# Planner delays of weight sums, down operands and norm statistics in a two-layer trunk

## The chip, the cores and the metric

The kernel runs on one core of one Trainium2 chip. The metric is the device time of one launch in microseconds (us). The kernel before has a median of 2538.11 us over 3 runs (2534.14 to 2538.69). One further execution was recorded by the hardware profiler; it took 2531.58 us, and its trace is what the rows below are read from.

## The reference, cut to what matters

Two layers work on `x` of 1024 tokens by 1024 channels in float32. Each layer adds three terms in turn: a mixer, an attention to a memory of 256 tokens, and a gated feed-forward block; a last RMSNorm ends the trunk.

```python
# even layer: short gated convolution beside causal pooling;  odd layer: mLSTM beside latent attention
x = x + mixer(rmsnorm(x, norm_mix_g))
x = x + memory_cross_attention(rmsnorm(x, norm_xattn_g), mem_n, wq, wkv, wo)
g, u = split(rmsnorm(x, norm_ffn_g) @ w_gate_up)     # 1024 -> 2 * 2816
x = x + (silu(g) * u) @ w_down                       # 2816 -> 1024
```

## The kernel before, in words

`x` stays on chip, transposed: 8 blocks of 128 channels for each of two token halves of 512. Every product of matrices is made of matmuls of 128 by 128 by 512, and each stands three times: operands are split in a high part (`whi` of a weight, `xgh`, `xth`, `fh` of an activation) and a low remainder (`wlo`, `xgl`, ...), and `mm3` (its matmuls are recorded at L267) adds high by high, high by low and low by high.

A weight takes a fixed path. SP loads a raw tile of 256 KB (`fetch`, L331) into one of five buffers `wraw`; ScalarE (ACT) writes `whi` (L344); VectorE (DVE) writes `wlo` = `wraw` - `whi` (L345), which frees the raw buffer for the next load. Some weights are sums of two tiles. Such a sum is an accumulating DMA on the queue of GpSimd (POOL), L339, onto a raw tile that is already there, either out of HBM (`in_ffn_...`) or out of another raw tile (`wraw<-wraw`). It starts when both tiles are there, and only when it has landed can ACT and DVE split the tile.

The feed-forward block runs 22 column blocks j in pairs of products by a form with seven products in place of eight. One period of two j's has three stages on TensorE (PE): a gate and up stage of 84 matmuls, G1 (j odd), another, G2 (j even), and the down stage D of 84 matmuls (`Down.out`), which adds into `x` by 28 DVE additions (L204), four for each of the seven products. In each stage two weights are loaded sums out of HBM (s1 and s3) and two are sums of these with other tiles (s2 after s1, s4 after s2). DVE and ACT also make, in the same stretch, the gate (L2038 copies a psum, L2042 scales, L2044 is SiLU, L2046 scales, L2053 multiplies by up) and the operands of the next down stage: `Down.build` forms seven right-hand operands `11`, `t1`, `t2`, `21`, `t3`, `22`, `t4` of two finished j's, and `parts` splits each by an ACT copy (L138) and a DVE subtraction (`fh`, L139). The products in D come in the order 11, 12, s2, s1, s3, s4, 22.

The order of instructions on each engine is written by a planner in Python (`Threads`). Parts of the program are generators that `yield` either a delay in planned nanoseconds or an event; a matmul moves the planner's clock on, and of the generators that are due the one with the lowest rank writes its next instructions. The delays decide only where an instruction stands in its engine's queue; on the chip each engine takes its queue in order and waits by semaphores. Three rules matter here. `pair_blocks.landed` says when a sum may be split while splits are still ahead of need: 4500 planned ns after its DMA was written for s2 and s4, 5500 for s1 and s3; if a product needs the weight, `must` splits at once. `self.ahead` is how many split weights may stand ready (3 inside the feed-forward block, 2 elsewhere). And `D1`, `D2` delay the statistics of a norm: `norm_stats` sums squares on PE (`ssq`), makes the reciprocal root by small DVE operations (L473 to L478), copies it to `ncol` (L530), and D2 later broadcasts it to rows on PE (`rbp`, L271) and ACT (`rb`, L537). The event `col_ev`, also D2 later, lets the cross attention start (L1827).

Around the FFN these rules act in three other places. In the even layer's mixer the pooling waits for `rb` (L790 on DVE, then a chain of POOL additions L796, then `pd` L805 on DVE, then the matmul `pps`). In the odd layer's mixer `rb` scales `qk` (L1247). In the cross attention, the attention itself and the down stage share DVE.

Of the kernel before, what the change touches and what calls it, by code (L numbers as in the profile page):

```python
# [115 lines left out]
class Down:  # L116
# [36 lines left out]
    def build(self, c):  # L153

        t = self.t

        def tile(i, h):
            while (c, i, h) not in self.full:
                yield 500
            return self.full[c, i, h]  # L160

        def operand(nm, src, fresh=True):
            if self.pace and fresh:
                yield self.pace / 2
            yield (self, 2)
            self.right[c, nm] = self.parts(src, self.eng)
            t.th.set(self.ev[c][nm], 2500)
            if self.pace:
                yield self.pace / 2 if fresh else self.pace

        b11 = yield from tile(0, 0)
        if self.pace:
            yield self.over[c - 1]
        yield from operand("11", b11, False)
        b12 = yield from tile(0, 1)
        t.nc.vector.tensor_sub(b11, b11, b12)
        yield from operand("t1", b11)
        b22 = yield from tile(1, 1)
        t.nc.vector.scalar_tensor_tensor(b11, b11, -1.0, b22, op0=ALU.mult, op1=ALU.subtract)
        yield from operand("t2", b11)  # L180
        b21 = yield from tile(1, 0)
        yield from operand("21", b21, False)
        t.nc.vector.tensor_sub(b12, b22, b12)
        yield from operand("t3", b12)
        yield from operand("22", b22, False)
        t.nc.vector.scalar_tensor_tensor(b11, b11, -1.0, b21, op0=ALU.mult, op1=ALU.subtract)
        yield from operand("t4", b11)

# [33 lines left out]
class Trunk:  # L222
# [4 lines left out]

    D1, D2, D3 = 15000, 6000, 20000  # L230
    PARTS = ((0, slice(0, HT)), (1, slice(0, 256)), (1, slice(256, HT)))
    BUFS = {"xg": 32, "g": 20, "o": 8, "p": 7, "pt": 4, "r": 4, "rb": 2}
    RAWS = 5
# [136 lines left out]
    def pair_blocks(self, order, eng):  # L370


        names, raw, step, at = deque(("s1", "11", "12", "s3", "22")), {}, {}, {}
        th = self.th
        reads = {"s1": 2, "11": 3, "12": 2, "s3": 1, "22": 1}

        def get(nm):
            while nm not in raw:
                self.fetch()
                raw[names[0]], step[names[0]], at[names[0]] = self.raws.popleft()  # L380
                names.popleft()
                self.held += 1
            return raw[nm]

        def read(nm):
            reads[nm] -= 1
            if not reads[nm]:
                self.held -= 1

        def add(nm, place, other):  # L390
            src = get(other)
            before = [step[other]] if step.get(other) else []
            step[nm] = step[place] = self.add_to(raw[place], src, 3500 if before else 1000, before)
            raw[nm] = raw[place]
            emit = step[nm].emit
            step[nm].emit = lambda: (emit(), read({"s2": "11"}.get(other, other)))

        def landed(nm):
            s = step.get(nm)
            if s is None:  # L400
                return th.now >= at[nm] + 3500
            return s.out is not None and th.now >= s.out + (4500 if nm in ("s2", "s4") else 5500)

        for nm in order:
            tile = get(nm)
            while not self.must and not landed(nm):
                yield None
            if step.get(nm):
                step[nm].flush()
            self.split_w(tile, eng)  # L410
            read({"s2": "11", "s4": "12"}.get(nm, nm))
            if nm == "11":
                add("s2", "11", "s1")
            elif nm == "12":
                add("s4", "12", "s2")
            yield False
# [83 lines left out]
    def late_stats(self, N, h, rows):  # L500

        nc, acc = self.nc, None
        yield 3000
        for t in self.xT[h]:
            sq = self.g("p" if acc else "pt", name="sq")
            nc.scalar.activation(sq, t, AF.Square)
            if acc is None:
                acc = sq
            else:
                nc.vector.tensor_add(acc, acc, sq)  # L510
            yield 800
        yield from self.norm_stats(N, h, acc, rows, (self.D1 if rows else self.D3) - 9400)

    def norm_half(self, N, h, gname, off=0, rows=True):

# [1739 lines left out]
```

## Time and profile before

| What | Value |
|---|---|
| median of 3 runs | 2538.11 us |
| the profiled execution | 2531.58 us, its span 2529.9 us |
| PE, matmuls | 2473.7 us busy, 98% of the span, 12029 instructions |
| DVE | 1955.1 us, 77% |
| ACT | 1082.3 us, 43% |
| POOL | 450.9 us, 18% |
| DMA, HBM read | 176.84 MB |

Busy time of matmuls overlaps, since they are pipelined: a matmul of 512 columns lasts about 0.39 us in the trace, and the next one starts about 0.23 us after it. A short wait of PE can therefore hide inside the busy time, and waits are read from the distance between starts. The chain that ended last is PE for 75%, DVE for 13% and DMA for 4%.

### The profile page before, as it was taken

The page shows a single profiled execution, that of the slowest core. Times are in us where ns is not written, and L with a number is a line of the kernel's source. Part 1 is how long each engine was busy: PE and PEld are TensorE (multiplying, and loading weights), DVE is VectorE, ACT ScalarE, POOL GpSimd, SP SyncE. Part 2 cuts the span into 40 slices and gives each one's busy share as a digit, 9 for nine tenths or more (in the row PEclk, how much of TensorE's full clock was granted, in tenths as well). Part 3 has the DMA queues.
Part 4 walks back from the last instruction along what each step waited for, and adds up shares of the span by engine and source line. Part 5 has one row for each costly group of instructions (what it writes and reads, how often), then busy time and mean ns, then how long its engine had stood idle before and what let it go on. Part 6 is the DMA issues. An engine that isn't in the chain of part 4 may idle for free.

```text
span 2529.9 us, 34429 instructions
## 1 busy us (share of the span) xinstructions
PE 2473.7 (98%) x12029; PEld 2027.8 (80%) x12029; DVE 1955.1 (77%) x3789; ACT 1082.3 (43%) x2125; POOL 450.9 (18%) x487
## 2 busy tenths in 40 slices
PE   9999999999999999999999999999999999999998
PEld 7788888777777777779998788788777777777777
DVE  5777779988888887774638788787998777888887
ACT  5322555533333333343324367575554333333333
POOL 5411021121222122110000120001111212121222
PEclk9999999999999999999999999999999999999999
DMA  5232212455555555511122132122135555555552
GB/s 139 54 83 81 92 47 58 87 120 121 118 122 117 115 125 122 116 42 39 39 50 55 31 81 72 46 84 51 45 80 122 118 115 117 117 122 120 119 119 97
DMA packets 300093, 227.33 MB, mean 90 GB/s; under 512 B 28911, under 2 KB 250320, under 8 KB 299920
## 3 DMA queue, kind: packets, MB, share of 16 engines
q1 hardware_dynamic: 226688, 150.28, 20.5%
q0 software_dynamic: 72912, 74.32, 18.9%
q8 instruction: 95, 1.56, 0.3%
q14 instruction: 78, 0.64, 0.1%
q10 hardware_dynamic: 320, 0.53, 0.1%
HBM read 176.84 MB, written 4.19 MB: 72 GB/s over the span
## 4 chain that ended last, share of the span: by engine, by line
PE 75%; DVE 13%; DMA 4%; issue 4%; ACT 3%; POOL 1%; SPq 0%; DVEq 0%; ACTq 0%; POOLq 0%
PE gu L267 25%; PE pj L267 14%; PE dn L267 12%; PE op L267 6%; DVE x L204 4%; PE tp L267 4%; DMA wraw<-wraw 3%; DVE wlo L345 3%; PE as L267 2%; PE ao L267 1%; DMA wraw<-in_ffn_w_down_dram 1%; DVE fh L139 1%; PE apt L271 1%; PE o L267 1%; PE kps L267 1%
## 5 line engine op out<-in xcount | busy, mean ns | idle before, releaser
L344 ACT CAST whi<-wraw 128x512 fp32r<-128x512 f32 (+1 forms) x652 | 398.8, 617 | 929.4 <-DMA wraw<-wraw 207.7
L345 DVE TENSOR_TENSOR wlo<-wraw,whi 128x512 fp32r<-128x512 f32 (+1 forms) x652 | 442.2, 686 | 176.4 <-ACT whi L344 170.4
L267 PE MATMUL dn<-fh,whi 128*128 128x512 f32 x1456 | 459.9, 397 | 14.7 <-DVE x L204 11.0
L204 DVE TENSOR_TENSOR x<-x,dn 128x512 f32<-128x512 f32 x728 | 451.5, 677 | 0.3 <-PE dn L267 0.2
L267 PEld LDWEIGHTS dn<-fh,whi 128*128 128x128 f32 x1456 | 266.1, 188 | 100.8 <-issue 22.8
L267 PE MATMUL dn<-fh,wlo 128*128 128x512 f32 x728 | 286.0, 393 | 0.0
L267 PE MATMUL gu<-xth,whi 128*128 128x512 f32 x672 | 267.2, 398 | 8.9 <-DVE f L2063 3.1
L267 PE MATMUL gu<-xtl,whi 128*128 128x512 f32 x672 | 264.9, 394 | 0.7 <-DVE xtl L286 0.7
L267 PE MATMUL gu<-xth,wlo 128*128 128x512 f32 x672 | 265.0, 394 | 0.0
L267 PE MATMUL pj<-xgh,whi 128*128 128x512 f32 x592 | 238.7, 403 | 2.1 <-DVE x L204 2.1
L267 PE MATMUL pj<-xgl,whi 128*128 128x512 f32 x592 | 231.3, 391 | 0.0
L267 PE MATMUL pj<-xgh,wlo 128*128 128x512 f32 x592 | 231.3, 392 | 0.0
L267 PE MATMUL gu<-xgh,whi 128*128 128x512 f32 x568 | 224.1, 394 | 0.2
L267 PE MATMUL gu<-xgh,wlo 128*128 128x512 f32 x568 | 222.0, 391 | 0.0
L267 PE MATMUL gu<-xgl,whi 128*128 128x512 f32 x568 | 221.7, 390 | 0.0
L339 POOL DMA_DIRECT2D wraw<-in_ffn_w_gate_up_dram x84 | 116.1, 1382 | 509.1 <-DVE x L204 119.6
L339 POOL DMA_DIRECT2D wraw<-wraw x136 | 124.9, 918 | 390.0 <-DVE wlo L345 141.4
L267 PEld LDWEIGHTS dn<-fh,wlo 128*128 128x128 f32 x728 | 136.7, 188 | 31.2
L267 PEld LDWEIGHTS gu<-xth,whi 128*128 128x128 f32 x672 | 126.7, 189 | 42.8 <-ACT f L2038 8.3
L267 PEld LDWEIGHTS gu<-xtl,whi 128*128 128x128 f32 x672 | 126.9, 189 | 29.2 <-DVE xtl L286 1.6
L267 PEld LDWEIGHTS gu<-xth,wlo 128*128 128x128 f32 x672 | 126.9, 189 | 29.1
L267 PEld LDWEIGHTS pj<-xgh,whi 128*128 128x128 f32 x592 | 111.7, 189 | 25.8 <-issue 2.7
(494 smaller groups left out, 4736.5 us busy)
## 6 DMA issues: line engine op xcount, KB each, us to landing
wraw<-in_ffn_w_gate_up_dram SPq DMA_DIRECT2D x218, 256.0 KB, 3.0
wraw<-wraw POOLq DMA_DIRECT2D x136, 256.0 KB, 3.4
wraw<-in_ffn_w_down_dram SPq DMA_DIRECT2D x108, 256.0 KB, 2.8
wraw<-in_ffn_w_gate_up_dram POOLq DMA_DIRECT2D x84, 256.0 KB, 5.1
wraw<-in_od_w_in_dram SPq DMA_DIRECT2D x42, 256.0 KB, 2.8
wraw<-in_ffn_w_down_dram POOLq DMA_DIRECT2D x40, 256.0 KB, 4.5
wraw<-in_ev_w_in_dram SPq DMA_DIRECT2D x32, 256.0 KB, 2.6
wraw<-in_xattn_wkv_dram SPq DMA_DIRECT2D x32, 256.0 KB, 2.7
```

Source lines behind the costliest of these rows:

```text
L139: eng.tensor_sub(lo, src, hi.bitcast(F32))
L204: getattr(nc.vector, op)(x, x, ps)
L267: self.nc.tensor.matmul(out, lhsT, rhs, start=start, stop=stop, skip_group_check=onto)
L271: self.nc.tensor.transpose(out, src, self.ident[:k, :k])
L339: return Step(self.th, lambda: self.nc.gpsimd.dma_start(out=raw, in_=src, accum_op=ALU.add), delay, before)
L344: self.nc.scalar.copy(hi, raw)
L345: (eng or self.nc.vector).tensor_sub(lo, raw, hi.bitcast(F32))
```

## The change

Delays of the planner change. No operation is added or taken away.

```diff
-        def operand(nm, src, fresh=True):
-            if self.pace and fresh:
+        def operand(nm, src):
+            if self.pace:
                 yield self.pace / 2
             yield (self, 2)
             self.right[c, nm] = self.parts(src, self.eng)
             t.th.set(self.ev[c][nm], 2500)
             if self.pace:
-                yield self.pace / 2 if fresh else self.pace
+                yield self.pace / 2
...
-        yield from operand("11", b11, False)
+        yield from operand("11", b11)
...
-    D1, D2, D3 = 15000, 6000, 20000
+    D1, D2, D3 = 15000, 8500, 20000
...
-            return s.out is not None and th.now >= s.out + (4500 if nm in ("s2", "s4") else 5500)
+            return s.out is not None and th.now >= s.out + (4500 if len(self.ready) < 2 else 8000)
...
-        yield from self.norm_stats(N, h, acc, rows, (self.D1 if rows else self.D3) - 9400)
+        yield from self.norm_stats(N, h, acc, rows, (self.D1 + 2500 if rows else self.D3) - 9400)
```

The operands `21` and `22` lose their third argument in the same way as `11`. With `pace` 2400, which only the feed-forward block sets, the plain operands are now written 1200 planned ns later, as the fresh ones were. A sum now has to be 8000 planned ns old if two split weights already stand ready, else 4500. `col_ev` and the broadcast of the norm come 2500 planned ns later, and so do the statistics of the odd layer's mixer norm.

What that does to the queues is seen at three places. The first is DVE in a steady down stage D of the first feed-forward block, from the first addition of its second product on (`x_..` are blocks of `x`, `dn` the psum tiles of D). Before:

```order
L204 TENSOR_TENSOR x_0_82<-x_0_82,dn 128x512
L204 TENSOR_TENSOR x_1_83<-x_1_83,dn 128x512
L204 TENSOR_TENSOR x_2_84<-x_2_84,dn 128x512
L204 TENSOR_TENSOR x_3_85<-x_3_85,dn 128x512
L139 TENSOR_TENSOR fh<-f,fh 128x512
L345 TENSOR_TENSOR wlo<-wraw,whi 128x512
L204 TENSOR_TENSOR x_0_90<-x_0_90,dn 128x512
L204 TENSOR_TENSOR x_1_91<-x_1_91,dn 128x512
L204 TENSOR_TENSOR x_2_92<-x_2_92,dn 128x512
L204 TENSOR_TENSOR x_3_93<-x_3_93,dn 128x512
L345 TENSOR_TENSOR wlo<-wraw,whi 128x512
```

After, from the same addition:

```order
L204 TENSOR_TENSOR x_0_82<-x_0_82,dn 128x512
L345 TENSOR_TENSOR wlo<-wraw,whi 128x512
L204 TENSOR_TENSOR x_1_83<-x_1_83,dn 128x512
L139 TENSOR_TENSOR fh<-f,fh 128x512
L204 TENSOR_TENSOR x_2_84<-x_2_84,dn 128x512
L204 TENSOR_TENSOR x_3_85<-x_3_85,dn 128x512
L204 TENSOR_TENSOR x_0_90<-x_0_90,dn 128x512
L204 TENSOR_TENSOR x_1_91<-x_1_91,dn 128x512
L139 TENSOR_TENSOR fh<-f,fh 128x512
L204 TENSOR_TENSOR x_2_92<-x_2_92,dn 128x512
L204 TENSOR_TENSOR x_3_93<-x_3_93,dn 128x512
L345 TENSOR_TENSOR wlo<-wraw,whi 128x512 x2
```

A second `fh` (L139), that of operand `22`, stands among the additions of D, where before it stood in G2. One `wlo` that stood just ahead of these rows now comes behind their first addition, and the `wlo` that followed the `fh` comes four additions later. The second place is the POOL queue in a G2 stage, the accumulating DMAs with the raw tiles that they write, 6447 being s1, 6453 s2, 6494 s3, 6468 s4 (after: 6443, 6449, 6508, 6467), and the two that follow for D. Before:

```order
L339 DMA wraw_6447<-in_ffn_w_gate_up_dram 128x4x128
L339 DMA wraw_6453<-wraw_6447 128x512
L339 DMA wraw_6494<-in_ffn_w_gate_up_dram 128x4x128
L339 DMA wraw_6468<-wraw_6453 128x512
L339 DMA wraw_6604<-in_ffn_w_down_dram 128x512
L339 DMA wraw_6639<-in_ffn_w_down_dram 128x512
```

After:

```order
L339 DMA wraw_6443<-in_ffn_w_gate_up_dram 128x4x128
L339 DMA wraw_6508<-in_ffn_w_gate_up_dram 128x4x128
L339 DMA wraw_6449<-wraw_6443 128x512
L339 DMA wraw_6467<-wraw_6449 128x512
L339 DMA wraw_6604<-in_ffn_w_down_dram 128x512
L339 DMA wraw_6655<-in_ffn_w_down_dram 128x512
```

The DMA of s3 now stands ahead of that of s2, the order that G1 and D have in both kernels. The third place is PE in the even layer's mixer, around the broadcast `rbp` of the norm's two halves (`pj` are the projection's psum tiles). Before:

```order
L267 MATMUL pj_607<-xgl_442,whi_520 128x512
L267 MATMUL pj_607<-xgh_441,wlo_521 128x512
L271 MATMUL rbp_632<-ident_73,ncol_550 128x128 x4
L267 MATMUL pj_660<-xgh_180,whi_573 128x512
L267 MATMUL pj_660<-xgl_181,whi_573 128x512
L267 MATMUL pj_660<-xgh_180,wlo_574 128x512
```

After:

```order
L267 MATMUL pj_632<-xgh_224,whi_573 128x512
L267 MATMUL pj_632<-xgl_225,whi_573 128x512
L267 MATMUL pj_632<-xgh_224,wlo_574 128x512
L271 MATMUL rbp_645<-ident_73,ncol_550 128x128 x4
L267 MATMUL pj_632<-xgh_240,whi_579 128x512
L267 MATMUL pj_632<-xgl_241,whi_579 128x512
```

The first broadcast moves behind `xgh_224`, 12 matmuls later than before, and the second one moves by 12 too.

## Rows read from the trace of the kernel before

**Rows 1.** The page's first lines: span, and PE's busy time.

```profile
span 2529.9 us, 34429 instructions
PE 2473.7 (98%) x12029; PEld 2027.8 (80%) x12029; DVE 1955.1 (77%) x3789; ACT 1082.3 (43%) x2125; POOL 450.9 (18%) x487
```

**Rows 2.** Stretches: start and end, length, then busy time (instructions) of each engine, clock.

```profile
740.20:799.30 59.10, 58.95 (x254) 46.91 (x253) 47.54 (x78) 21.72 (x38) 12.00 (x12) 1.00 0.57 121
978.50:1037.10 58.60, 58.60 (x253) 46.95 (x252) 46.53 (x77) 21.40 (x37) 11.66 (x12) 1.00 0.59 122
```

**Rows 3.** Timeline of PE, one stage D: start, length, then the wait before it.

```profile
740.24 0.63 PE L267 MATMUL dn<-fh,whi 128*128 128x512 f32 x2
760.25 0.47 PE L267 MATMUL gu<-xgh,whi 128*128 128x512 f32 x1
```

**Rows 4.** Timeline of DVE, the same stage D and what stands ahead.

```profile
739.45 0.69 DVE L345 TENSOR_TENSOR wlo<-wraw,whi 128x512 fp32r<-128x512 f32 x1 [1.09 <-ACT whi L344]
742.65 1.87 DVE L204 TENSOR_TENSOR x<-x,dn 128x512 f32<-128x512 f32 x3
759.42 4.86 DVE L204 TENSOR_TENSOR x<-x,dn 128x512 f32<-128x512 f32 x8
764.81 1.28 DVE L345 TENSOR_TENSOR wlo<-wraw,whi 128x512 fp32r<-128x512 f32 x2
```

**Rows 5.** Timeline of ACT: the splits of two sums (s2 of D, s2 of the next G2).

```profile
738.79 0.62 ACT L344 CAST whi<-wraw 128x512 fp32r<-128x512 f32 x1 [3.44 <-DMA wraw<-wraw]
...
779.05 0.62 ACT L344 CAST whi<-wraw 128x512 fp32r<-128x512 f32 x1 [4.35 <-DMA wraw<-wraw]
```

**Rows 6.** Timeline of POOL, the accumulating DMAs: s3 and s2 of D; s2 of the next G2.

```profile
733.39 0.88 POOL L339 DMA_DIRECT2D wraw<-in_ffn_w_down_dram  x1 [5.28 <-DVE wlo L345]
733.95 1.21 POOL L339 DMA_DIRECT2D wraw<-wraw  x1
...
775.53 0.89 POOL L339 DMA_DIRECT2D wraw<-wraw  x1 [5.03 <-DVE f L2070]
```

**Rows 7.** Timeline of DVE, the splits that free raw buffers for SP.

```profile
705.28 1.28 DVE L345 TENSOR_TENSOR wlo<-wraw,whi 128x512 fp32r<-128x512 f32 x2
...
729.36 0.68 DVE L345 TENSOR_TENSOR wlo<-wraw,whi 128x512 fp32r<-128x512 f32 x1
```

**Rows 8.** Timeline of DVE: the longest such wait, second layer's block.

```profile
1966.92 0.69 DVE L345 TENSOR_TENSOR wlo<-wraw,whi 128x512 fp32r<-128x512 f32 x1 [3.34 <-ACT whi L344]
```

**Rows 9.** Timeline, even layer's mixer: broadcast, pooling, and the product that waits.

```profile
51.82 0.60 PE L271 MATMUL rbp<-ident,ncol 128*128 128x128 f32 x4
...
57.69 0.91 POOL L339 DMA_DIRECT2D wraw<-in_ev_w_out_dram  x1
...
76.57 0.18 DVE L803 TENSOR_TENSOR pd<-psum,recip 128x16 f32<-128x16 f32 x1 [1.70 <-POOL psum L796]
...
86.45 0.67 DVE L805 SCALAR_TENSOR_TENSOR pd<-psum,pz 128x512 f32<-128x512 f32 x1
...
87.27 1.10 PE L267 MATMUL pps<-pd,poolw 128*128 128x512 f32 x2 [0.95 <-DVE pd L805]
```

**Rows 10.** Timeline, odd layer's mixer: small norm operations, `qk`, and the broadcast.

```profile
1125.35 0.68 DVE L1247 SCALAR_TENSOR_TENSOR qk<-pj,rb 128x512 f32<-128x512 f32 x1
...
1128.58 0.17 DVE L530 COPY ncol<-ny 128x4 f32<-128x4 f32 x1
...
1128.80 1.02 PE L271 MATMUL rbp<-ident,ncol 128*128 128x128 f32 x4 [3.57 <-DVE ncol L530]
```

**Rows 11.** The stretch behind it, columns as in rows 2.

```profile
1130.00:1150.00 20.00, 20.00 (x119) 16.27 (x117) 4.85 (x12) 4.81 (x7) 0.00 (x0) 0.94 0.11 27
```

**Rows 12.** First cross attention: 30 us ahead of its stage D, and D.

```profile
345.00:375.00 30.00, 29.32 (x165) 24.12 (x164) 24.26 (x57) 21.07 (x58) 11.33 (x12) 1.00 0.10 19
375.00:408.40 33.40, 32.52 (x166) 25.95 (x164) 31.65 (x66) 18.47 (x45) 7.02 (x7) 1.00 0.13 40
```

**Rows 13.** The page's costly groups: weight loads of gate and up that wait for ACT.

```profile
L267 PEld LDWEIGHTS gu<-xth,whi 128*128 128x128 f32 x672 | 126.7, 189 | 42.8 <-ACT f L2038 8.3
```

More of the change, by code (lines that the diff above doesn't have):

```diff
@@ L181, in build @@
         b21 = yield from tile(1, 0)
-        yield from operand("21", b21, False)
+        yield from operand("21", b21)
         t.nc.vector.tensor_sub(b12, b22, b12)
         yield from operand("t3", b12)
-        yield from operand("22", b22, False)
+        yield from operand("22", b22)
         t.nc.vector.scalar_tensor_tensor(b11, b11, -1.0, b21, op0=ALU.mult, op1=ALU.subtract)
```

## Prediction

> **What bounds the kernel now.** I began with the page's first part. It puts PE at 98% of the span [rows 1], which looks like a kernel that only fewer matmuls can shorten. But that busy time counts overlap, so I went on to the table of stretches, the timelines and the order of instructions, and asked in each place that the change touches who waits for whom.
>
> A period of the feed-forward block is 252 matmuls. In the stretch of 59.10 us PE is busy 58.95 us with 254 records [rows 2], 0.232 us each; that is an estimate of PE's own pace and from above, since the short waits are in it. A stage D of 84 would take 19.5 us at that pace; the one that I looked at lasts from 740.24 to 760.25, 20.0 us [rows 3]. The shortest period is 58.60 us [rows 2].
>
> What sets the place of D is seen on DVE. The last `wlo` ahead of the stage waits 1.09 us for `whi` [rows 4], and ACT started that `whi` only when a DMA of the kind `wraw<-wraw` had landed [rows 5]. Of the 18 steady stages (9 in each block) every one has such a wait; 1.09 us is the shortest and 3.34 us the longest [rows 4, 8]. From the first addition at 742.65 on DVE then runs without a gap to the splits that start at 764.81 [rows 4]. Those splits free raw buffers, SP loads into them, POOL adds to what was loaded, and the sum is split again. I followed the ring through one period: a `wlo` in G1 from 705.28 frees a buffer, two chained sums later a `whi` is split in G2, 13 DVE operations later a `wlo` at 729.36 frees the next buffer [rows 7], and the two sums of D behind it end in the `whi` at 738.79 [rows 5] and the additions at 742.65 [rows 4]. From 705.28 to the same place, 764.81, is 59.5 us, and PE is no part of it. So the steady periods go by a ring of DVE and DMA which is about 1 us slower than PE; PE hides most of it.
>
> **The change part by part.** Durations are from the profiled execution of 2531.58 us, whose span is 2529.9 us [rows 1]. The median of the runs is 2538.11, 6.5 us above it. I add the sum to the median, since that is what the kernel after will be measured by. A measurement of this kernel tells about 0.2%, 5.1 us, from no change.
>
> *Operands written later.* In the steady D stages the additions get one more `fh` in their midst. The gap-free row has one operation every 0.60 us (8 in 4.86 us, the last one's own 0.68 taken off [rows 4]). PE leaves D when the 21st addition frees its psum tile, 0.60 us later than before if the first addition keeps its time. Does it? The ring holds 38 operations from the first addition to the `wlo` that frees the buffer for G2's sums, before as after: what D gains, the next G1 loses. Thus the ring keeps its length, PE comes into the next stage 0.60 us later and waits 0.60 us less for it, and every steady stage has at least 1.09 us of such a wait to give. Without that cover each of 18 stages would cost 0.60, 10.8 us. The tenth stage of each block also goes from 11 to 12 operations among the additions and has no ring behind it: 2 x 0.60 = +1.2 us. Range 0 to +10.8.
>
> *Splits of the sums.* In steady periods the splits stand where they stood, an operation or so apart; those of s2, which the ring waits for, do not move against it. POOL's s3 now stands ahead of s2 in G2. The row for s2 with s3 ahead by 0.56 us is D's: issued 733.95, split at 738.79, 4.84 us. Without it, in G2, it is 775.53 to 779.05, 3.52 us [rows 5, 6]. After the change s3 would go out as soon as its base tile is there, over 2 us ahead of s2, which still waits for s1. I take 0, nearer to the second row; the upper bound is 1.3 us in each of 18 periods. ACT's copies L2038 stand a little earlier in G2; the PE waits that they end are 8.3 us in all [rows 13], but in stretches that the ring times, so I take 0 here as well, with -8.3 as the end on the other side.
>
> *Broadcast later, even layer's mixer.* `rbp` moves behind 12 matmuls, 12 x 0.232 = 2.8 us, from 51.82 [rows 9]. POOL's pooling chain starts behind it; one DMA of 0.91 us at 57.69 [rows 9] goes ahead of the chain instead of standing in it, so the chain ends 1.9 to 2.8 us later. DVE's L803 at 76.57 waits 1.70 us for that chain, and 12 operations later (12 in the new order too) comes the `pd` of 86.45, for which PE waits 0.95 us at 87.27 [rows 9]. PE's work up to there is the same, so the delay arrives whole. I take +2.0. Lower bound 0, if gaps of DVE in between give way; upper bound 2.8 and a fall of the clock (below), 4.0.
>
> *Odd layer's mixer.* PE waits 3.57 us for `ncol` before the second broadcast [rows 10], and the granted clock of the next 20 us is 0.94 [rows 11]: it ran at 1.2 instead of 2.4 GHz for about 2.4 us and lost 1.2 us. The first broadcast, 0.6 us by the same four in rows 9, falls into that wait from now on. But the DVE chain gets longer: the two `qk` of 0.68 [rows 10] stay in it and a `wlo` of 0.6 joins. Sum 0, bounds -1.2 and +1.2.
>
> *Cross attention.* It starts 12 matmuls later, so 6 more of its DVE operations come into the stage D that it shares (44 in place of 38 among the additions). There DVE is busy 31.65 of 33.40 us with 66 operations, 0.48 us each [rows 12]; the 30 us ahead have 5.7 us of idle DVE which the six leave unused. 6 x 0.48 = 2.9, less the 1.75 us that D has idle, is 1.1 us, in two layers +2.2. Bounds: +5.8 if the idle time cannot be used; -1.4 if the 0.68 us that PE lacks in the 30 us ahead [rows 12] goes, twice.
>
> *Head of each feed-forward block.* PE's order is the same there, and DVE has as many operations up to the first addition: 0.
>
> Sum: 1.2 + 0 + 2.0 + 0 + 2.2 + 0 = +5.4 us, in the profiled run's terms 2537.0, against the median 2543.5 us.
>
> **The rivals.**
>
> *R1, the ring is not closed.* If the first addition comes later when PE does, since the gate's last operations need PE's psum, each steady stage pays: 10.8 + 5.4 = +16.2, 2554. For it: the shortest period, 58.60, is nearly all PE. Against it: all 18 waits for the DMA, which must be under 0.6 us before it decides.
>
> *R2, the DMAs get in each other's way.* s3's accumulation is in flight while s1's is, and s2 starts late. If half of the 1.3 us between the two rows comes in each period: 0.65 x 18 = 11.7, with the rest +17.1, 2555. The ring has no slack, so it decides from the first tenth of a microsecond on. Against it: the shorter row, and G1, which has this order already.
>
> The Trainium skill, "DMA: Bandwidth & Descriptors", section on issuing engines that are not separate queues, says that transfers from SP and POOL run on the same 16 engines and interleave, whichever engine issued them. By that rule s3's transfer takes from s1's time, and R2 is the result; the 4.84 against 3.52 us agree with it.
>
> *R3, faster.* ACT and DVE no longer sit at the head of their queues with a split whose sum has not landed, and the copies behind it come in time. If the PE waits for L2038 go (-8.3), the mixer's delay is hidden in DVE's gaps (0) and the attentions gain nothing nor lose: -8.3 + 1.2 = -7.1, 2531. For it: the waits stand in a row of the page. Against it: a wait of PE that goes inside a ring's period comes back in the next D. It decides if the ring shortens by some 0.4 us a period, for which the order gives no reason.
>
> *R4, nothing lasts.* Both later starts are absorbed: +1.2, 2539.
>
> **How the numbers follow.** Forecast 0.45, and its own range, from the mixer at 0 and the attentions at 0 to both at 4.0, is +1.2 to +9.2; it straddles the bound, and I split it into 0.21 slower and 0.24 no change. R1 0.10 and R2 0.10, both slower. R3 0.27, faster. R4 0.08, no change. That makes faster 0.27, same 0.32, slower 0.41. The likeliest time is 2543.5. A range that holds 8 in 10 reaches from R3's 2531 to R2's 2555; I take 2530 to 2556.
>
> **What would show it.** Right: the wait of the `wlo` ahead of D is still there and about as long, D lasts 0.6 us longer from PE's side in steady stages while the periods stay at 58.6 to 61; the wait for `pd` near 88 us is 2 to 4 us; D of the attentions lasts about 34 us. R1: the wait ahead of D is gone and periods are 0.6 us longer. R2: from issue to `whi`, s2 of G2 takes over 4 us. R3: periods are shorter. The forecast is wrong if the period's mean moves by over 0.3 us in either direction.

## The result, and the profile after

The kernel after took 2558.91 us, the median of 5 runs (2557.42 to 2560.15), against 2538.11 for the kernel before (5 runs beside it, 2532.79 to 2538.69). The ratio is 1.0088, interval 1.0074 to 1.0101: slower by about 22 us. The forecast was 2543.5 in a range that ended at 2556, so time and range both missed it.

The profiled execution of after took 2560.15 us. It is the slowest of its five, and the profiled execution of before (2531.58 us) lies below all of its runs, so the two traces are 28.5 us apart where the medians are 20.8 apart. Prices below are taken from medians, places from the traces. The page of after, against [rows 1]:

```profile
span 2558.4 us, 34455 instructions
PE 2487.1 (97%) x12029; PEld 2024.1 (79%) x12029; DVE 1957.9 (77%) x3789; ACT 1078.2 (42%) x2126; POOL 450.4 (18%) x487
```

Where in the program the time went is read by the start of the same stage D in both traces. Each feed-forward block has nine steady periods from its first D to its last. The table of stretches over these nine periods, columns as in [rows 2], before (first layer, second layer):

```profile
499.50:1037.10 537.60, 532.14 (x2269) 421.99 (x2268) 429.26 (x704) 196.08 (x343) 110.60 (x109) 1.00 0.58 120
1905.30:2445.20 539.90, 532.35 (x2269) 421.81 (x2268) 429.28 (x704) 196.10 (x343) 110.64 (x109) 1.00 0.57 119
```

and after:

```profile
502.80:1056.80 554.00, 540.06 (x2270) 419.65 (x2269) 431.14 (x702) 193.10 (x343) 110.02 (x108) 1.00 0.56 116
1925.60:2473.10 547.50, 535.61 (x2269) 420.76 (x2268) 431.05 (x702) 193.89 (x343) 110.03 (x108) 1.00 0.57 117
```

The first layer's block starts 3.3 us later and loses 16.4 us in its nine periods; the second's loses 7.6. That is 24.0 of the 28.5 us: the mean period goes from 59.86 to 61.19 us (the sums of the lengths over 18). The even mixer gives 4.2 us. So the steady periods, which the forecast took to keep their length, hold nearly all of it.

One steady period of after, in the views of [rows 2 to 4]: two periods in the table of stretches, then PE and DVE in the stage D that starts at 748.62.

```profile
748.60:810.40 61.80, 60.19 (x253) 46.57 (x252) 47.90 (x78) 21.35 (x38) 12.21 (x12) 1.00 0.56 116
995.60:1056.80 61.20, 59.87 (x254) 46.70 (x253) 47.38 (x77) 21.04 (x38) 12.21 (x12) 1.00 0.56 116
```

```profile
748.62 0.63 PE L267 MATMUL dn<-fh,whi 128*128 128x512 f32 x2
771.68 0.47 PE L267 MATMUL gu<-xgh,whi 128*128 128x512 f32 x1
```

```profile
750.27 0.69 DVE L345 TENSOR_TENSOR wlo<-wraw,whi 128x512 fp32r<-128x512 f32 x1 [3.54 <-ACT whi L344]
753.48 1.87 DVE L204 TENSOR_TENSOR x<-x,dn 128x512 f32<-128x512 f32 x3
763.66 1.28 DVE L345 TENSOR_TENSOR wlo<-wraw,whi 128x512 fp32r<-128x512 f32 x2
```

D lasts 23.06 us on PE (20.01 before), and the `wlo` ahead of the additions waits 3.54 us for a sum (1.09 before, which was the shortest wait of the 18; in the mean of the 18 it goes from 1.86 to 2.66 us). DVE comes to its additions later, and PE waits for it inside D. The sums come late; the next view asks which.

The queues of SP and POOL in the G1 that follows, before (first addition of D at 742.65 [rows 4]). In order: SP's fourth load of this stage, then the DMAs of s3, s2 and s4, then SP's first loads for G2.

```profile
750.55 0.37 SPq L331 DMA_DIRECT2D wraw<-in_ffn_w_gate_up_dram  x1
...
754.08 1.29 POOL L339 DMA_DIRECT2D wraw<-in_ffn_w_gate_up_dram  x1 [6.43 <-DVE wlo L345]
756.80 0.89 POOL L339 DMA_DIRECT2D wraw<-wraw  x1 [1.44 <-DVE wlo L345]
760.79 0.86 POOL L339 DMA_DIRECT2D wraw<-wraw  x1 [3.10 <-DVE x L204]
...
765.52 2.17 SPq L331 DMA_DIRECT2D wraw<-in_ffn_w_gate_up_dram  x3
```

The same five after (first addition at 753.48):

```profile
764.40 0.37 SPq L331 DMA_DIRECT2D wraw<-in_ffn_w_gate_up_dram  x1
...
768.07 1.29 POOL L339 DMA_DIRECT2D wraw<-in_ffn_w_gate_up_dram  x1 [9.43 <-DVE wlo L345]
768.82 1.45 POOL L339 DMA_DIRECT2D wraw<-wraw  x1
774.82 0.86 POOL L339 DMA_DIRECT2D wraw<-wraw  x1 [4.55 <-DVE x L204]
...
779.01 2.66 SPq L331 DMA_DIRECT2D wraw<-in_ffn_w_gate_up_dram  x5
```

Read against the first addition, the load goes from +7.90 to +10.92 us, s3 from +11.43 to +14.59, s2 only from +14.15 to +15.34, s4 from +18.14 to +21.34, and the loads for G2 from +22.87 to +25.53. The means over the 18 periods say the same, worked out from each DMA's issue and landing. The last row counts periods by D's first addition; by D's first matmul they are the 59.86 and 61.19 us above.

| from the first addition of D, us | before | after |
|---|---|---|
| SP, fourth load of G1 (base of s3) | 8.10 | 11.06 |
| POOL, s3 of G1 issued | 11.67 | 14.77 |
| POOL, s2 of G1 issued, landed | 14.36, 17.70 | 15.52, 20.65 |
| POOL, s4 of G1 issued, landed | 18.32, 22.32 | 21.35, 24.68 |
| SP, first load of G2 | 23.08 | 24.85 |
| POOL, s2 of G2 landed | 36.63 | 37.73 |
| POOL, s2 of D landed | 55.99 | 57.40 |
| next first addition | 59.94 | 61.37 |

This is theory A. The new `landed` rule moves s4's `wlo` in D four additions back, and the second `fh` now stands ahead of it too. That `wlo` frees the raw buffer into which SP loads the base of G1's s3. POOL takes its queue in order and s3 stands ahead of s2 there, so s2 is issued 1.2 us later, and then takes 5.1 us in place of 3.3, since s3's transfer now runs 0.75 us ahead of it and no longer 2.7. s4 adds s2's raw tile, and until s4's DMA has read that tile SP cannot load G2's first tile into it; before, the last to hold that buffer was DVE's own split of s2. In the trace of after SP's load comes 0.14 us after s4's landing in 16 of the 18 periods; in that of before it comes 0.03 us after the end of a `wlo` in 17 of them. The places further down in the table are 1.1 to 1.8 us later than before.

Two rivals had to be told apart from it. B: the additional `fh` in D is paid in every stage, as in R1. C: the DMAs of G2, where s3 now stands ahead of s2, slow each other, as in R2.

### The profile page after: what moved, and what is told of

Its sections match the earlier page's. It is cut to its first block, busy times and chain, and to the rows that moved or that the text cites. A ratio compares the mean times of both kernels' runs of the same rounds, so it can differ in the third digit from the quotient of the medians.

```text
span 2558.4 us, 34455 instructions
## 1 busy us (share of the span) xinstructions
PE 2487.1 (97%) x12029; PEld 2024.1 (79%) x12029; DVE 1957.9 (77%) x3789; ACT 1078.2 (42%) x2126; POOL 450.4 (18%) x487
## 4 chain that ended last, share of the span: by engine, by line
PE 68%; DVE 17%; DMA 6%; issue 5%; ACT 2%; POOL 1%; SPq 0%; DVEq 0%; POOLq 0%; ACTq 0%
PE gu L267 22%; PE pj L267 14%; PE dn L267 9%; DVE x L204 6%; PE op L267 6%; DVE wlo L345 4%; PE tp L267 4%; DMA wraw<-wraw 3%; PE as L267 2%; DVE fh L139 1%; PE ao L267 1%; DMA wraw<-in_ffn_w_down_dram 1%; PE apt L271 1%; PE o L267 1%; ACT whi L344 1%
## 5 line engine op out<-in xcount | busy, mean ns | idle before, releaser
L344 ACT CAST whi<-wraw 128x512 fp32r<-128x512 f32 (+1 forms) x652 | 395.1, 616 | 957.6 <-DMA wraw<-wraw 316.5
L345 DVE TENSOR_TENSOR wlo<-wraw,whi 128x512 fp32r<-128x512 f32 (+1 forms) x652 | 445.0, 689 | 188.5 <-ACT whi L344 184.7
L267 PE MATMUL dn<-fh,whi 128*128 128x512 f32 x1456 | 464.7, 400 | 29.2 <-DVE x L204 26.2
L267 PEld LDWEIGHTS dn<-fh,whi 128*128 128x128 f32 x1456 | 262.9, 188 | 128.4 <-DVE x L204 29.9
L267 PE MATMUL dn<-fh,wlo 128*128 128x512 f32 x728 | 285.9, 393 | 0.0
L267 PE MATMUL gu<-xth,whi 128*128 128x512 f32 x672 | 267.6, 398 | 6.7 <-DVE f L2063 2.5
L267 PE MATMUL gu<-xtl,whi 128*128 128x512 f32 x672 | 265.3, 395 | 0.5 <-DVE xtl L286 0.5
L267 PE MATMUL gu<-xth,wlo 128*128 128x512 f32 x672 | 265.6, 395 | 0.0
L267 PE MATMUL pj<-xgh,whi 128*128 128x512 f32 x592 | 239.5, 405 | 2.1 <-DVE x L204 2.1
L267 PE MATMUL pj<-xgl,whi 128*128 128x512 f32 x592 | 232.0, 392 | 0.0
L267 PE MATMUL pj<-xgh,wlo 128*128 128x512 f32 x592 | 231.7, 392 | 0.0
L267 PE MATMUL gu<-xgh,whi 128*128 128x512 f32 x568 | 223.5, 394 | 0.2
L267 PE MATMUL gu<-xgh,wlo 128*128 128x512 f32 x568 | 222.2, 391 | 0.0
L267 PE MATMUL gu<-xgl,whi 128*128 128x512 f32 x568 | 222.2, 391 | 0.0
L339 POOL DMA_DIRECT2D wraw<-in_ffn_w_gate_up_dram x84 | 109.4, 1303 | 580.9 <-DVE wlo L345 229.3
L339 POOL DMA_DIRECT2D wraw<-wraw x136 | 136.3, 1002 | 346.5 <-DMA wraw<-wraw 145.7
L267 PEld LDWEIGHTS dn<-fh,wlo 128*128 128x128 f32 x728 | 136.6, 188 | 31.1
L267 PEld LDWEIGHTS gu<-xth,whi 128*128 128x128 f32 x672 | 126.5, 188 | 41.3 <-ACT f L2038 8.4
L267 PEld LDWEIGHTS gu<-xtl,whi 128*128 128x128 f32 x672 | 127.0, 189 | 29.6 <-DVE xtl L286 1.3
L267 PEld LDWEIGHTS gu<-xth,wlo 128*128 128x128 f32 x672 | 126.9, 189 | 29.4
L267 PEld LDWEIGHTS pj<-xgh,whi 128*128 128x128 f32 x592 | 112.0, 189 | 26.3 <-issue 2.7
```

The source lines that it names most:

```text
L267: self.nc.tensor.matmul(out, lhsT, rhs, start=start, stop=stop, skip_group_check=onto)
L339: return Step(self.th, lambda: self.nc.gpsimd.dma_start(out=raw, in_=src, accum_op=ALU.add), delay, before)
L344: self.nc.scalar.copy(hi, raw)
L345: (eng or self.nc.vector).tensor_sub(lo, raw, hi.bitcast(F32))
```

## Experiments

Each ratio is against the kernel before in runs beside it, with its 95% interval.

**only_s4**: the kernel before, with the later split for s4 alone. One `wlo` per stage D moves back four additions; PE's order is that of before.

```diff
-            return s.out is not None and th.now >= s.out + (4500 if nm in ("s2", "s4") else 5500)
+            return s.out is not None and th.now >= s.out + (4500 if nm == "s2" or nm == "s4" and len(self.ready) < 2 else 8000 if nm == "s4" else 5500)
```

> The kernel before with one delay changed: the sum s4 is split only when it is 8000 planned ns old if two split weights stand ready. In each steady D stage one wlo moves behind four additions; PE's order is the same. Theory A (that wlo frees the raw buffer for the fourth load of the next G1, and POOL's s3, s2 and s4 queue behind that load): fourth SP load at 11 us after the first addition in place of 8, period 61 to 61.5 us in place of 59.9, +18 to +26 us, about 2560. Rival B (the operand 22 among the additions of D makes the loss) and rival C (the order s3 before s2 in G2): no change here, within 5 us of 2538.

Measured 2549.83 us, ratio 1.0050 (1.0038 to 1.0063). One DVE operation that changes places with four others costs 0.5%, over half of the whole loss. That is 12.7 us, less than the 18 to 26 that theory A had given, and more than the 5 that its rivals allowed. POOL's queue in its trace (first addition at 749.03) shows the chain of after: s3 at +13.96, s2 0.76 behind it, s4 at +20.57.

```profile
762.99 1.29 POOL L339 DMA_DIRECT2D wraw<-in_ffn_w_gate_up_dram  x1 [8.95 <-DVE wlo L345]
763.75 1.45 POOL L339 DMA_DIRECT2D wraw<-wraw  x1
769.60 0.86 POOL L339 DMA_DIRECT2D wraw<-wraw  x1 [4.40 <-DMA wraw<-wraw]
```

**s4_as_before**: the kernel after, with s4 split by the short delay again.

```diff
-            return s.out is not None and th.now >= s.out + (4500 if len(self.ready) < 2 else 8000)
+            return s.out is not None and th.now >= s.out + (4500 if len(self.ready) < 2 or nm == "s4" else 8000)
```

> The kernel after, with s4 alone split at 4500 planned ns again; operands, norm delays, the split of the other sums and PE's order are as in the kernel after. Theory A: fourth load back at about 8 us, periods 59.5 to 60.2 us, what is left is the even mixer's delay, 2538 to 2545. Rivals B and C: the periods stay at 61.4 us, about 2557.

Measured 2552.78 us, ratio 1.0057 (1.0044 to 1.0069). About a third of the loss of after (0.88%) goes, less than the 0.50% that the move costs alone; 0.57% stays. That is neither the 2538 to 2545 us of theory A nor the 2557 of its rivals, so there is more to find.

**only_operand** and **only_norm**: the kernel before, with the change of `operand` alone, and with the change of `D2` and of the odd norm's `D1` alone (their diffs stand above).

> The kernel before with the operands alone written later (a second fh among the additions of D, s3 ahead of s2 on POOL in G2). Theory A and the record's step that the ring keeps its length: -2 to +4 us. Rival B: +11 us or more. Rival C: +12 us or more, with s2 of G2 over 4 us from issue to split.

> The kernel before with the two norm delays alone (col_ev and the broadcast 2500 planned ns later, the odd mixer's statistics 2500 later). The feed-forward blocks' order is as before. Expected: even mixer +4.2 us as in the trace of the kernel after, cross attentions -1 to +2 each, so +2 to +7 in all. If the norm delays make the loss of 20 us: over +12.

Measured 2546.03 us, 1.0031 (1.0021 to 1.0042), and 2542.74 us, 1.0017 (1.0008 to 1.0025). The norms' price is inside its range. That of the operands lies between the +4 us at which theory A ended and the +11 and +12 at which B and C began; the sign of C came, with s2 of G2 at 4.05 us from issue to split in the mean (3.51 before). The three parts alone make 0.50 + 0.31 + 0.17 = 0.98%, against 0.88% together: they nearly add up, and operands and norms together, 0.48%, are most of what s4_as_before has left. The nine periods of each block with the operand change alone are longer by 9.1 and 1.0 us than before in the traces.

```profile
500.40:1047.10 546.70, 536.45 (x2269) 420.58 (x2268) 431.13 (x702) 196.18 (x343) 109.77 (x108) 1.00 0.57 118
1914.80:2455.70 540.90, 535.21 (x2270) 421.26 (x2269) 431.17 (x702) 196.18 (x343) 109.83 (x108) 1.00 0.57 119
```

**s4_g1_s2**: only_s4, and in G1 the DMA of s3 is put behind that of s2 in POOL's queue. This tests the link of theory A: the load of s3's base stays late, but s2 and s4 no longer stand behind it. The same edit serves the kernels that follow; `late` is set for the sums of G1, G2 or D. `second` is the last s2 that was written, and `issue_after` puts s3 behind it in POOL's queue. An s3 that is `late` may also be split as soon as its DMA is written. The added lines move the line numbers: L339 stands at L343, L344 and L345 at L354 and L355, L267 at L268.

```diff
-            step = more is not None and self.add_to(raw, more, 3500)
+            step = more is not None and self.add_to(raw, more[0], 14000 if more[1] else 3500, late=more[1])
...
+        def emit():
+            behind = self.tc.issue_after(self.second.ins) if late and self.second is not None else ExitStack()
+            with behind:
+                ins = self.nc.gpsimd.dma_start(out=raw, in_=src, accum_op=ALU.add)
+            if before and before[0].first:
+                self.second = ins
```

> The kernel only_s4 (late split of s4) with one more change: in G1 stages the accumulating DMA of s3 is queued on POOL behind that of s2, so s2 and s4 do not wait for s3's late base tile nor share the DMA engines with it. SP's loads and PE's order stay. Theory A with POOL's queue as the link: SP's fourth load still at 10.5 us, but s4 of G1 lands near 22 us after the first addition in place of 24.1, G2's first load returns to 23.1, time 2536 to 2543. If the late split costs in another way (the split itself, SP's load of s3, the product s3): stays at 2547 to 2553.

Measured 2536.07 us, ratio 0.9993 (0.9984 to 1.0001): the loss of 0.5% is gone. Its POOL queue (first addition at 745.20) has s2 at +14.16, s3 behind it and s4 at +18.19, as early as before, although SP's fourth load is as late as 10.49 us after the first addition in the mean. SP's first load of G2 is back at +23.09 in the mean (23.08 before, 24.28 in only_s4).

```profile
759.36 0.88 POOL L343 DMA_DIRECT2D wraw<-wraw  x1 [9.17 <-DVE wlo L355]
759.90 1.67 POOL L343 DMA_DIRECT2D wraw<-in_ffn_w_gate_up_dram  x1
763.39 0.88 POOL L343 DMA_DIRECT2D wraw<-wraw  x1 [1.82 <-DVE x L204]
```

So the late `wlo` does no harm by itself; what it delays is s3, and s3 delays s2 and s4 by its place in the queue. Theory A is shown for the sums. The swap in G1 alone on the kernel before was not run; that it gives back what was lost and nothing beyond is read from the means, where s2 lands at +17.81 and s4 at +22.57 (17.70 and 22.32 before).

**op_g2_s2**: only_operand, with s3 behind s2 in G2, as a test of C.

> The kernel only_operand with s3's accumulating DMA behind that of s2 on POOL in G2 stages, as in the kernel before; nothing else moves. Rival C, which only_operand left open: s2 of G2 takes 3.4 in place of 3.95 us from issue to landing, and the 8 us lost fall to 0 to 3, 2537 to 2541. If the second fh in D costs them (rival B): no change, 2543 to 2548.

Measured 2542.42 us, 1.0021 (1.0011 to 1.0031); its runs spread from 2536.86 to 2551.46. Against the 1.0031 of only_operand the intervals overlap, and the median lies between the two ranges. In the trace, which is that of its slowest run, s2 of G2 takes 3.44 us again in place of 3.95, but s1 ahead of it takes 6.18 in place of 5.67, and s2 lands at +37.31, no earlier than the +37.01 of only_operand. This does not settle what C is worth.

**op11_21**: the kernel before, with operands 11 and 21 later and 22 as it was. D keeps its one `fh`; G2 has the new order of s3 and s2.

```diff
-        yield from operand("11", b11, False)
+        yield from operand("11", b11)
...
-        yield from operand("21", b21, False)
+        yield from operand("21", b21)
```

> The kernel before with operands 11 and 21 alone written later; 22 keeps its place, so D has one fh among the additions as before, while G2 queues s3 ahead of s2 on POOL as in only_operand. If the second fh in D costs the 8 us of only_operand (B): 2536 to 2541. If they come from where 11 and 21 put the splits and the DMAs: 2543 to 2548.

Measured 2533.29 us, 0.9982 (0.9973 to 0.9991): slightly faster, and below both ranges, on the side of B. From here to only_operand it is operand 22 alone, and that costs 0.49%, 12.4 us, 0.69 us in each of 18 periods, about one DVE operation of 0.60 us. In op11_21 the stretch from the first addition to G1's split of s2 has one operation fewer than before, and SP's first load of G2 comes at +22.59 in place of +23.08 us; yet G2's s2 lands no earlier (36.60 against 36.63), since it takes 3.83 us in place of 3.41 from issue to landing with s3's transfer ahead of it. So 22 gives the ring back the operation that 11 and 21 took out of it, and what only_operand pays on balance is of the size of those 0.4 us, 0.42 x 18 = 7.6 against the 0.31%, 7.9 us. This is argued from counts and sizes, and not shown. That op_g2_s2 did not win them back tells little, since s2 of G2 landed no earlier there; the share of C is open.

**down_s2**, **g1down_s2** and **after_s2**: s3 behind s2 in D alone on the kernel before; in D and G1; and in all three stages on the kernel after.

> The kernel before with s3's accumulating DMA behind that of s2 on POOL in D's sums alone. If the ring of DVE and DMA sets the period, s2 of D lands 1.5 to 2 us earlier (3.4 in place of 4.9 us from issue to landing, and 0.5 earlier issue), the wait of the wlo ahead of D goes under 0.7 us, and the period falls from 59.9 to 58.6 us, where PE takes over: -12 to -22 us, 2515 to 2526. If PE sets the period: within 4 us of 2537.

> As down_s2, and in G1 too s3 queues behind s2. In the kernel before G1's s2 and s4 land about when DVE gets to the split, so a further 0 to -5 us against down_s2, by SP's first load of G2 coming earlier. If s3 of G1 becomes late for its product: up to +10 us against down_s2.

> The kernel after, with s3's accumulating DMA queued on POOL behind that of s2 in every stage of the feed-forward blocks. If all that the change costs there goes through the ring of DVE and DMA, and that ring falls below PE's own pace as in down_s2, the whole loss in the feed-forward blocks goes with it and the norm delays' 4 us remain: 2505 to 2514. If the operands or the late split cost PE something else too (B): above 2516.

Measured 2504.35 us (2502.64 to 2505.11), 0.9869 (0.9856 to 0.9881); 2504.55 us, 0.9873 (0.9859 to 0.9887); 2510.41 us, 0.9889 (0.9875 to 0.9902). The first beats both kernels, by 34 and 55 us, more than the 12 to 22 that were expected; G1's swap adds nothing to it, and after_s2 is inside its range. In the traces PE, ACT, DVE and SP take the same instructions in the same order in down_s2 as in before (by operation and tile); the order of POOL's DMAs alone differs. Its D in the views of [rows 3 to 6] (the first addition is at 736.11): POOL issues s2, then s3; ACT splits s2.

```profile
728.60 0.87 POOL L343 DMA_DIRECT2D wraw<-wraw  x1 [5.56 <-DVE wlo L355]
729.13 1.22 POOL L343 DMA_DIRECT2D wraw<-in_ffn_w_down_dram  x1
```

```profile
732.13 0.62 ACT L354 CAST whi<-wraw 128x512 fp32r<-128x512 f32 x1 [2.13 <-PE gu L268]
```

```profile
732.31 0.69 DVE L2090 TENSOR_TENSOR f<-f,gu 128x512 f32<-128x512 f32 x1 [1.39 <-PE gu L268]
732.92 0.69 DVE L355 TENSOR_TENSOR wlo<-wraw,whi 128x512 fp32r<-128x512 f32 x1
```

From issue to split s2 takes 3.53 us (4.84 before, [rows 5, 6]), ACT's `whi` now waits for PE and not for a DMA, and the `wlo` has no wait left (0.28 us in the mean of 18, 1.86 before). A period is then PE's own:

```profile
499.70:1024.70 525.00, 523.59 (x2269) 424.72 (x2269) 430.52 (x705) 196.88 (x344) 111.03 (x109) 1.00 0.60 123
1892.30:2420.30 528.00, 525.11 (x2270) 424.10 (x2269) 430.30 (x705) 196.13 (x344) 111.08 (x109) 1.00 0.60 122
734.90:793.10 58.20, 58.19 (x254) 47.21 (x252) 47.77 (x78) 21.74 (x38) 12.20 (x12) 1.00 0.60 122
```

58.5 us in the mean against 59.86. PE is busy for 523.59 of 525.00 us, and g1down_s2, whose DMAs stand otherwise in G1, comes to 58.6 us as well. With the same queue order on the kernel after, the nine periods cost no more than that:

```profile
505.20:1032.10 526.90, 525.64 (x2269) 424.36 (x2268) 430.71 (x704) 198.66 (x344) 111.42 (x109) 1.00 0.60 122
1897.20:2424.70 527.50, 526.11 (x2270) 424.07 (x2269) 430.91 (x704) 197.51 (x344) 111.52 (x109) 1.00 0.60 122
```

So none of the loss of after in the feed-forward blocks is paid by PE itself, the operands' part included, although the second `fh` still stands among the additions of D: it goes when s2 stands ahead of s3. That does not show that every part came from the order of those two DMAs, since a ring that is faster than PE hides its other delays too. The 6 us that after_s2 is above down_s2 are about the price of the norms (0.17%, 4.3 us).

**down_s2_D4000**: down_s2 with `D2 = 4000`, norms earlier than before.

> down_s2 with the norm's broadcast and the cross attention 2000 planned ns earlier (D2 4000 in place of 6000), the other way round from the change. Even mixer: the wait for pd, 0.95 us, goes, and the attentions' D ends up to 1 us earlier: -1 to -4 us against down_s2, 2500 to 2504. If an earlier broadcast makes PE wait for ncol: up to +4.

Measured 2505.64 us, 0.9866 (0.9853 to 0.9880): no difference to down_s2, and not the gain of 1 to 4 us that was expected. In the trace PE's wait for `pd`, which was to go, is 3.3 us (0.97 in down_s2), and the even mixer's D starts 3.9 us later (108.67 against 104.78); at the end nothing of it is left, the spans being 2503.0 and 2503.4 us. The mixer is thus slower by some 4 us with 4000 as with 8500, and a step from 6000 in neither direction won any time.

## Why the prediction was wrong, point by point

*Splits of the sums: the step that failed.* It took 0, because the splits "stand where they stood, an operation or so apart", and those of s2 do not move. The `wlo` that moves by four additions stood in the order of DVE ahead of the prediction, but the prediction asked only whether a split that the ring waits for moves, which is s2's. A split also frees a raw buffer, and what loads into that one was not followed: SP's fourth load, s3, and behind s3 in POOL's queue s2 and s4. Measured, +0.50% or 12.7 us alone (only_s4), and 0.31% when it is taken back from the kernel after (s4_as_before). By the prediction's own sign, a mean period that moves by over 0.3 us, it was wrong: the period moved by 1.3. The ring that the prediction described is real; this link of it was left out. The 1.3 us between an s2 with s3 close ahead and one without [rows 5, 6] was the price of this mechanism, asked for G2 only; in G1 s2 came to take 1.8 us longer. G1 "has this order already" (R2) was no reason: there s3 stood 2.7 us ahead, and the change brought it to 0.75.

*Operands later: taken +1.2, measured +0.31%, 7.9 us*, inside its bounds of 0 to +10.8. That the ring keeps its count of DVE operations agrees with op11_21, where it loses one and gains. What the count leaves out is time that is not DVE's. By the flights in G2 it is at least partly s2 behind s3 (3.95 us in only_operand and 3.83 in op11_21, against 3.41), which the prediction had among the splits, at 0; how much of the 7.9 us that makes is open.

*Even mixer: taken +2.0, measured +4.2 in the trace*, just above its upper bound of 4.0. The mechanism was right and mis-sized. The rows of after, against [rows 9]:

```profile
78.84 0.17 DVE L803 TENSOR_TENSOR pd<-psum,recip 128x16 f32<-128x16 f32 x1 [1.70 <-POOL psum L796]
...
89.07 0.69 DVE L805 SCALAR_TENSOR_TENSOR pd<-psum,pz 128x512 f32<-128x512 f32 x1
...
89.91 1.35 PE L267 MATMUL pps<-pd,poolw 128*128 128x512 f32 x2 [3.96 <-DVE pd L805]
```

The pooling chain ends 2.3 us later and the second `pd` 2.6, the upper end of the 1.9 to 2.8 given. PE then waits 3.96 us in place of 0.95, and its granted clock behind the wait is 0.83 over 10 us, where before it was 1.00:

```profile
87.30:97.30 10.00, 10.00 (x43) 7.94 (x43) 4.63 (x8) 3.38 (x5) 5.02 (x7) 1.00 0.40 79
```

```profile
90.00:100.00 10.00, 10.00 (x36) 7.61 (x37) 5.05 (x8) 2.66 (x4) 3.48 (x5) 0.83 0.23 52
```

0.17 of 10 us are 1.7 us lost, 3.4 us at 1.2 in place of 2.4 GHz. 2.6 and 1.7 make 4.3, about the shift of D. The fall of the clock was seen as possible and kept out of the value, though the same trace showed one behind a wait of 3.57 us [rows 10, 11].

*Cross attention: taken +1.1 each, measured -0.9 in the first layer and -0.2 in the second*, to the last addition of its D. The stage D does what was worked out. In the timeline of its matmuls (count, ns, first and last start) before and after:

```profile
L267 PE MATMUL dn<-fh,whi x56: 387/393/501, 375.2 to 407.7; 128*128 128x512 f32 x56
```

```profile
L267 PE MATMUL dn<-fh,whi x56: 387/391/482, 377.6 to 411.0; 128*128 128x512 f32 x56
```

From first to last start it is 32.5 and 33.4 us, +0.9 (taken +1.1). But the stage starts only 2.4 us later where the mixer had left it 4.1 behind, so 1.7 us were won ahead of it; the prediction had that gain as a bound of 0.7 and took nothing.

*Odd mixer: taken 0 in -1.2 to +1.2.* The wait for `ncol` is 3.72 us (3.57 before, [rows 10]) and the stage D behind it comes 1.2 us later than the block ahead had left it, the end of the range. *Head of the block: 0*, measured +0.1 in the first layer and -1.9 in the second, which is not explained. *L2038:* its waits are 8.4 us (8.3 before, [rows 13]): nothing went, and R3 fell with it.

*The rivals.* R2 named the mechanism, two accumulating DMAs close together with s2 the second, and its 2555 is the nearest time; its place was wrong for most of the loss, and its sign did not come in the kernel after, where s2 of G2 takes 3.65 us from issue to split and not over 4. The Trainium skill, "DMA: Bandwidth & Descriptors", section "Issuing engines are not separate DMA queues", says that DMAs run on the same 16 engines and interleave, whichever engine started them. The traces agree that a neighbour costs time, and show beyond it that the second one pays more: s2 of D took 4.92 us from issue to landing in the mean with s3 ahead and 3.63 us when it was put first. R1 expected the wait ahead of D to vanish; it grew, from 1.86 to 2.66 us in the mean.

## What to carry to other kernels

When a split or a copy moves in its queue, follow the buffer that it frees as well as the value that it makes: to the load that waits for the buffer, and then along the queue in which that load's follower stands. In a queue that is taken in order, a transfer that nobody needs soon must not stand ahead of one that a ring waits for; here the swap of two DMAs per period was worth 34 us. A ring with a small wait in every round has no slack, whatever share the busiest engine shows.

## What was not expected of the hardware

The means of the 18 periods give what an accumulating DMA of 256 KB between raw tiles took from issue to landing. It was 3.3 us when the other one on POOL's queue had been issued 2.7 us ahead, 3.6 to 4.0 when it had been issued 2.0 to 2.5 us ahead, 4.7 to 5.2 when 0.5 to 0.8 us ahead, and 3.4 to 3.6 when the other one followed it by 0.5 to 1.1 us: the one issued first keeps most of its speed.
